# The opening of a decoder step on one core: the third and fourth block of x are read ahead, the first gate weights are cast on VectorE, and two warming products go

## The chip, the cores and the metric

The kernel runs on one NeuronCore of one Trainium2 chip. Time is the device time of one execution in microseconds (us). Three runs of the kernel before gave 2344.27 (the median), 2343.6 and 2344.78 us. One more execution was taken with the hardware profiler; all lines of the profile come from it. Engines are named as the profile names them: PE is TensorE (PEld its weight loads), ACT is ScalarE, DVE is VectorE, POOL is GpSimd, SP is SyncE, which issues most DMAs.

## What is computed

One layer of a hybrid decoder on 304 tokens: 16 meta tokens, 256 of a prompt and 8 x 4 of a sample group. Cut to what matters:

```
def swiglu(x, w_gate, w_up, w_down):
    return (jax.nn.silu(x @ w_gate) * (x @ w_up)) @ w_down

x = x + 0.5 * swiglu(rmsnorm(x, norm_ffn1[l]), ffn1_w_gate[l], ffn1_w_up[l], ffn1_w_down[l])
m, hn, rn, im_ = mixer(rmsnorm(x, norm_mix[l]), l, hists[l], hres[l], hims[l], pos0)
x = x + m
x = x + 0.5 * swiglu(rmsnorm(x, norm_ffn2[l]), ffn2_w_gate[l], ffn2_w_up[l], ffn2_w_down[l])
```

D_MODEL is 2048, the FFN is 5632 wide, all numbers are fp32. The change touches only the start of the first line with `x + 0.5 * swiglu`: the norm of x and the first 256 columns of `x @ w_gate` and `x @ w_up`.

## The kernel before

**Exact products from rounded ones.** Each fp32 operand is split into a high part, rounded to the type fp32r, and a low part, the rest. A product of two such operands is three matmuls on PE: high by high, high by low, low by high (`mm3`, L241 to L243). ACT makes the high parts (for weights `whi`, for x `X` in L302), DVE the low ones (`wlo`, and `X` in L310). Activations lie with features on the 128 partitions and the 304 tokens along the free axis, so x has 16 rows of k ("tiles" of 128 features), four to a block: `pk` holds block 0, `xc1` to `xc3` the others (the profile writes `xc` for all three).

**The stream of weights.** Weights come in pieces of 4 rows of k by 256 columns, 512 KB each, in one fixed order for the whole program. `load` (L130, on SP) reads a piece into a ring of three `raw` slots; `high` (L152, ACT) and `low` (L161, DVE) split it into rings of four buffers; the slot is free when `low` is done, a buffer when PE has used it. `step` does `high`, `low` and `load` for one piece each. Pieces are numbered here in the order in which they are used: in the opening 0, 2, 4, 6 are gate and 1, 3, 5, 7 up; 8 to 11 are the gate weights of the next 256 columns.

**The opening** (`opening`, from L387) begins before anything is on the chip. Its work:

- SP reads `pk` in four transfers, one for each row of k: the norm's gain, the row of x, and pieces 0 and 1 for that row (L394). A part of the first transfer is read by ACT's queue (L396), `vec` too (L398). Then SP reads piece 2, block 1 of x in two halves (L402), pieces 3 and 4, and `hc` (L201).
- `stir` has PE multiply ones by ones STIR times; nothing reads the result. The profile counts two PE instructions for each.
- For each row of `pk`, `norm.add` makes the high and low part of x, and `parted` (L133 to L146) those of the two weight pieces for this row, the high ones with L143 on ACT, the low ones with L144 on DVE. `mms0` (L434) is the first row's 12 matmuls, in the order high by high, high by low, low by high.
- Then come four chunks of 48 matmuls, each a block of x with a gate and an up piece. After each half chunk `norm.add` is called for two rows of the next block, and `step` for the next pieces. Block c + 2 of x is read by SP in chunk c after the gate half (L465), at that place in SP's list.
- `squares` sums the squares of x for the norm: ACT squares a whole block (L418, L421), DVE adds (L422 to L426). PE turns the sums over (`ss`, L340) while the gate weights of the next 256 columns run, after pieces 8 and 9. The result is needed only then, since the norm's factor is multiplied in after the products.

Each engine works through its list in order, so an instruction that waits holds up all behind it. SP's list is such a list too: a read that waits for a `raw` slot holds up every read behind it.

Of the kernel before, what the change touches and what calls it, by code (L numbers as in the profile page):

```python
# [20 lines left out]
KD = D // P  # L21
# [6 lines left out]
NT = NMETA + NPR + NB * NS  # L28
# [4 lines left out]
KC = 4  # L33
# [11 lines left out]
NTV = 16 + NA  # L45
POOLRATE = 3.5
LATE = 8
STIR = 9
LAG = 2
ROWS = 15  # L50
MAGIC = 12582912.0
# [4 lines left out]
GC = 16  # L56
# [19 lines left out]
def nm(g, s):  # L76
    g.uid += 1
    return f"{s}_{g.uid}"
# [35 lines left out]
class Weights:  # L114
# [15 lines left out]
        g.nc.sync.dma_start(self.raw[i], src)  # L130
        self.loaded += 1

    def parted(self, i, k, src=None):  # L133

        nc = self.g.nc
        src = self.raw[i][:, k] if src is None else src
        if k == 0:
            self.parts[i] = tuple(self.pool.tile([P, KC, 256], F32R, tag=x, name=nm(self.g, x), bufs=AHEAD + 2)
                                  for x in ("whi", "wlo"))
            self.nhi += 1  # L140
            self.nlo += 1
        hi, lo = self.parts[i]
        nc.scalar.copy(hi[:, k], src)  # L143
        nc.vector.tensor_tensor(lo[:, k], src, hi[:, k].bitcast(F32), ALU.subtract)  # L144
        if k == KC - 1:
            self.raw.pop(i, None)  # L146
# [47 lines left out]
def tables(g):  # L194
    g.ident = g.const.tile([P, P], F32, name="ident")
    make_identity(g.nc, g.ident)


def masks(g):
    g.hc = g.const.tile([P, NT + NTV], F32, name="hc")  # L200
    g.nc.sync.dma_start(g.hc, g.I["consts"])  # L201
# [7 lines left out]
def step(g):  # L209

    g.w.high()
    flush(g)
    g.w.low()
    g.w.load()
    g.owed += g.rate
    while g.owed >= 1.0:
        g.owed -= 1.0
        got = next(g.side, None) if g.side is not None else None
        if got is None:
            g.side = None  # L220
# [18 lines left out]
def mm3(g, ps, wh, wl, x, start, stop):  # L239
    mm = g.nc.tensor.matmul  # L240
    mm(ps, wh, x[0], start=start, stop=False)  # L241
    mm(ps, wh, x[1], start=False, stop=False)  # L242
    mm(ps, wl, x[0], start=False, stop=stop)  # L243


def warm(g, func, pool=None):

    t = (pool or g.act).tile([P, 16 if pool else 1], F32, tag="warm", name=nm(g, "warm"))
    g.nc.scalar.activation(t[:, :1], g.ones[:, :1], func)


def bank(g, name, aux=False, pool=None):
    return (pool or (g.psaux if aux else g.psum)).tile([P, 512], F32, tag="ps", name=nm(g, name))
# [126 lines left out]
def stir(g):  # L380

    ps = bank(g, "stir", aux=True)
    for _ in range(STIR):
        g.nc.tensor.matmul(ps[:, :P], g.ones, g.ones, start=True, stop=True)


def opening(g, norm, xc, pk, sqp):  # L387

    nc, x, src = g.nc, g.x, g.I["xt"]
    names = ("ffn1_w_gate", "ffn1_w_up")  # L390
    cut = GC + NT + 256
    for k in range(KC):
        c1 = PKW if k else cut
        nc.sync.dma_start(pk[:, k, :c1], g.I["first"][k, :, :c1])  # L394
        if k == 0:
            nc.scalar.dma_start(pk[:, k, cut:], g.I["first"][k, :, cut:])  # L396
    warm(g, AF.Silu, g.const)
    nc.scalar.dma_start(g.vec, g.I["vec"])  # L398
    g.w.loaded = 2
    g.w.load()  # L400
    for h in range(2):
        nc.sync.dma_start(xc[1][:, 2 * h:2 * h + 2], src[1][:, 2 * h:2 * h + 2])  # L402
    g.w.load()
    g.w.load()
    tables(g)
    masks(g)
    stir(g)
    for k in range(KC):
        norm.add(x[k:k + 1], False, gain=pk[:, k, 0:1])
        for i in range(2):  # L410
            g.w.parted(i, k, pk[:, k, GC + NT + 256 * i:GC + NT + 256 * (i + 1)])
    pss = [[bank(g, "pj")[:, :norm.n] for _ in range(2)] for _ in range(2)]
    sums = sqp.tile([P, KC, NT], F32, name="sums")

    def squares(c):

        if c == 0:
            nc.scalar.activation(sums, xc[c], AF.Square)  # L418
            return
        sq = sqp.tile([P, KC, NT], F32, tag="sqs", name=nm(g, "sqs"))  # L420
        nc.scalar.activation(sq, xc[c], AF.Square)  # L421
        nc.vector.tensor_tensor(sums, sums, sq, ALU.add)  # L422
        if c == KD // KC - 1:
            nc.vector.tensor_tensor(sums[:, :2], sums[:, :2], sums[:, 2:], ALU.add)
            norm.acc = sums[:, 0]
            nc.vector.tensor_tensor(norm.acc, sums[:, 0], sums[:, 1], ALU.add)  # L426

    def mms0(ws):

        for w, y in ((0, 0), (0, 1), (1, 0)):  # L430
            for u in range(2):
                for f in range(2):
                    fs = slice(f * P, (f + 1) * P)
                    nc.tensor.matmul(pss[u][f], ws[u][w][:, 0, fs], norm.x[0][y], start=w == y == 0, stop=False)  # L434

    def mms(c, u, ws, kk):
        for f in range(2):
            fs = slice(f * P, (f + 1) * P)
            k = c * KC + kk
            mm3(g, pss[u][f], ws[u][0][:, kk, fs], ws[u][1][:, kk, fs], norm.x[k], k == 0, k == KD - 1)  # L440

    for c in range(KD // KC):
        if c == 0:
            ws = [g.w.take(name, 0, KC, 0) for name in names]
            mms0(ws)
            for kk in range(1, KC):
                for u in range(2):
                    mms(c, u, ws, kk)
        for u in range(2):
            if c:  # L450
                ws = [None, None]
                ws[u] = g.w.take(names[u], c * KC, KC, 0)
                for kk in range(KC):
                    mms(c, u, ws, kk)
            k = (c + 1) * KC + 2 * u
            if k < KD:
                norm.add(x[k:k + 2], False)
            if c == 0 and u == 0:
                for kk in range(KC):
                    g.w.parted(2, kk)  # L460
                g.w.load()
            else:
                step(g)
            if u == 0 and c + 2 < KD // KC:
                nc.sync.dma_start(xc[c + 2], src[c + 2])  # L465
            if c == 3 and u == 0:
                g.w.high()
                g.w.low()
                g.w.load()
            if c and u:  # L470
                squares(c - 1)
    return pss, squares
# [816 lines left out]
def body(ctx, tc, I, O):  # L1289
# [6 lines left out]
    with ExitStack() as c1:  # L1296
        xpool = c1.enter_context(tc.tile_pool(name="xp1", bufs=1))
        fpool = c1.enter_context(tc.tile_pool(name="ffn1", bufs=1))
        g.parts["H"] = (fpool, 4 * FC)
        pk = xpool.tile([P, KC, PKW], F32, name="pk")  # L1300
        xc = [pk[:, :, GC:GC + NT]] + [xpool.tile([P, KC, NT], F32, name=f"xc{c}") for c in range(1, KD // KC)]
        g.x = [xc[m // KC][:, m % KC] for m in range(KD)]
        sqs = ExitStack()
        sqp = sqs.enter_context(tc.tile_pool(name="sqs", bufs=1))
        opened = opening(g, n1, xc, pk, sqp)

        def started():
            sqs.close()
            g.side, g.rate = ssm_setup(g), SETRATE

        late = []

        def done(ms):
            n2.add([g.x[k] for k in ms], late=late if ms[0] >= LATE else None)
            for k in ms:
                nc.gpsimd.dma_start(xsc[k], g.x[k][:, NMETA:])

        g.started = started
        ffn(g, fpool, n1, 1, "H", done, opened)
        flush(g)  # L1320
        drain(g)
        ps0 = proj(g, "w_in", 0, n2.x, NT, KD, lambda c: [late.pop(0)() for _ in range(min(len(late), 2))])
        g.post.append(n2.begin)
# [67 lines left out]
```

## Time and profile before

| | |
|---|---|
| runs, median (lowest, highest) | 2344.27 us (2343.6, 2344.78) |
| profiled execution | 2344.06 us |
| its span, first to last instruction | 2342.3 us |
| PE busy | 2325.2 us, 99% of the span |
| DVE, ACT, POOL busy | 1582.5, 976.8, 87.7 us |
| DMA | 429.98 MB, mean 184 GB/s |

The page gives busy time by engine and groups of instructions by line. The timeline gives, for each row, start and length in us, the engine, line and operation, the tile written and those read, and in brackets how long the engine had been idle and what released it. An "SPq" row is the issue of a DMA, not its transfer. A table by stretch gives for a window the busy time and count of each engine, then PE's clock share, the DMA share and GB/s.

### The profile page before, as it was taken

How to read it: one execution, taken by the hardware profiler on the slowest of the kernel's cores; microseconds unless marked ns; L12 is line 12 of the kernel's file. 1: busy time of each engine (PE TensorE's matmuls, PEld its weight loads, DVE VectorE, ACT ScalarE, POOL GpSimd, SP SyncE). 2: the span in 40 equal slices, each digit the busy share in tenths (PEclk: the TensorE clock that was granted, in tenths of full speed). 3: DMA queues.
4: the chain of work that ended last, by engine and by line, in shares of the span. 5: the costliest groups of instructions: out<-in, count | busy, mean ns of one | idle time of the engine just before them, and what ended most of it. 6: DMA issues, size and time to landing. Idle time of an engine off the chain costs nothing.

```text
span 2342.3 us, 42290 instructions
## 1 busy us (share of the span) xinstructions
PE 2325.2 (99%) x17391; PEld 2306.2 (98%) x17391; DVE 1582.5 (68%) x2415; ACT 976.8 (42%) x1432; POOL 87.7 (4%) x160
## 2 busy tenths in 40 slices
PE   9999999999999999999999999999999999999997
PEld 8999999999999999999999999999999999999997
DVE  6788777877554558699999766555555555555655
ACT  5333433333533335445454544433333333333334
POOL 0000000001000002100000130000000000000000
PEclk9999999999999999999999999999999999999999
DMA  5444555556644445556666674444444444444443
GB/s 210 164 161 172 206 203 206 190 200 200 221 167 161 154 161 206 196 199 224 227 236 212 204 266 162 168 163 170 163 167 167 165 169 164 164 167 167 167 164 111
DMA packets 119361, 429.98 MB, mean 184 GB/s; under 512 B 14532, under 2 KB 19024, under 8 KB 119160
## 3 DMA queue, kind: packets, MB, share of 16 engines
q1 hardware_dynamic: 106800, 375.64, 46.0%
q0 software_dynamic: 12080, 51.45, 6.5%
q8 instruction: 136, 2.23, 0.4%
q14 instruction: 57, 0.47, 0.1%
q10 hardware_dynamic: 288, 0.19, 0.0%
HBM read 397.64 MB, written 29.95 MB: 183 GB/s over the span
## 4 chain that ended last, share of the span: by engine, by line
PE 97%; DMA 1%; DVE 1%; ACT 1%; issue 0%; SPq 0%; ACTq 0%; DVEq 0%
PE pj L241 24%; PE pj L242 24%; PE pj L243 24%; PE dn L243 8%; PE dn L241 8%; PE dn L242 8%; DMA xc<-in_xt 1%; PE bu L896 1%; PE yps L911 1%; DVE wlo L161 0%; DMA raw<-in_ffn_w_gate 0%; ACT whi L152 0%; DVE sums L422 0%; PE ss L340 0%; PE bt L839 0%
## 5 line engine op out<-in xcount | busy, mean ns | idle before, releaser
L161 DVE TENSOR_TENSOR wlo<-raw,whi 128x1024 fp32r<-128x1024 f32 x695 | 848.8, 1222 | 566.6 <-ACT whi L152 564.9
L152 ACT CAST whi<-raw 128x1024 fp32r<-128x1024 f32 x695 | 729.6, 1051 | 1135.5 <-PE pj L242 705.0
L241 PE MATMUL pj<-X,whi 128*128 128x304 f32 (+1 forms) x2428 | 731.3, 301 | 2.1 <-ACT whi L152 1.6
L243 PE MATMUL pj<-X,wlo 128*128 128x304 f32 (+1 forms) x2428 | 727.8, 300 | 1.4 <-DVE wlo L161 1.4
L242 PE MATMUL pj<-X,whi 128*128 128x304 f32 (+1 forms) x2428 | 728.1, 300 | 0.0
L242 PE MATMUL pj<-Y,whi 128*128 128x288 f32 x1728 | 510.2, 295 | 0.0
L241 PE MATMUL pj<-Y,whi 128*128 128x288 f32 x1728 | 510.0, 295 | 0.0
L243 PE MATMUL pj<-Y,wlo 128*128 128x288 f32 x1728 | 509.3, 295 | 0.0
L241 PEld LDWEIGHTS pj<-X,whi 128*128 128x128 f32 x2428 | 457.1, 188 | 8.6 <-issue 5.6
L243 PEld LDWEIGHTS pj<-X,wlo 128*128 128x128 f32 x2428 | 456.4, 188 | 2.2 <-DVE wlo L161 1.9
L242 PEld LDWEIGHTS pj<-X,whi 128*128 128x128 f32 x2428 | 456.6, 188 | 0.0
L241 PEld LDWEIGHTS pj<-Y,whi 128*128 128x128 f32 x1728 | 325.2, 188 | 2.0 <-issue 2.0
L242 PEld LDWEIGHTS pj<-Y,whi 128*128 128x128 f32 x1728 | 325.0, 188 | 0.0
L243 PEld LDWEIGHTS pj<-Y,wlo 128*128 128x128 f32 x1728 | 324.5, 188 | 0.0
L243 PE MATMUL dn<-H,wlo 128*128 128x304 f32 x704 | 213.0, 303 | 0.0
L241 PE MATMUL dn<-H,whi 128*128 128x304 f32 x704 | 213.0, 303 | 0.0
L242 PE MATMUL dn<-H,whi 128*128 128x304 f32 x704 | 212.2, 301 | 0.0
L242 PE MATMUL dn<-X,whi 128*128 128x288 f32 x704 | 207.7, 295 | 0.0
L241 PE MATMUL dn<-X,whi 128*128 128x288 f32 x704 | 207.5, 295 | 0.0
L243 PE MATMUL dn<-X,wlo 128*128 128x288 f32 x704 | 207.4, 295 | 0.0
L242 PEld LDWEIGHTS dn<-H,whi 128*128 128x128 f32 x704 | 132.4, 188 | 0.0
L242 PEld LDWEIGHTS dn<-X,whi 128*128 128x128 f32 x704 | 132.4, 188 | 0.0
(269 smaller groups left out, 1842.0 us busy)
## 6 DMA issues: line engine op xcount, KB each, us to landing
raw<-in_ffn_w_down SPq DMA_DIRECT2D x176, 512.0 KB, 3.5
raw<-in_ffn_w_gate SPq DMA_DIRECT2D x175, 512.0 KB, 3.5
raw<-in_ffn_w_up SPq DMA_DIRECT2D x175, 512.0 KB, 3.5
raw<-in_w_in SPq DMA_DIRECT2D x96, 512.0 KB, 4.0
raw<-in_w_out SPq DMA_DIRECT2D x32, 512.0 KB, 4.0
esc<-ee POOLq DMA_DIRECT2D x16, 912.0 KB, 5.8
ee<-esc POOLq DMA_DIRECT2D x16, 912.0 KB, 6.4
raw<-in_w_branch_a SPq DMA_DIRECT2D x16, 512.0 KB, 3.5
```

The costliest lines, as they stand in the source:

```text
L152: self.g.nc.scalar.copy(hi, self.raw[i])
L161: self.g.nc.vector.tensor_tensor(lo, raw, hi.bitcast(F32), ALU.subtract)
L241: mm(ps, wh, x[0], start=start, stop=False)
L242: mm(ps, wh, x[1], start=False, stop=False)
L243: mm(ps, wl, x[0], start=False, stop=stop)
L896: g.nc.tensor.matmul(ps, self.bs[i][rows, b, ri], self.up[u][rows], start=n == 0, stop=n == 2)
L911: g.nc.tensor.matmul(self.yps[i][q * 32:q * 32 + 32], c[:, h, q], s["k"][h][:, jj, NMETA:], start=k == 0, stop=k == 2)
```

## The change

```
-STIR = 9
+STIR = 7
...
-    def parted(self, i, k, src=None):
+    def parted(self, i, k, src=None, first=False):
...
-        nc.scalar.copy(hi[:, k], src)
+        (nc.vector.tensor_copy if first else nc.scalar.copy)(hi[:, k], src)
...
     g.w.load()
+    nc.sync.dma_start(xc[2], src[2])
     g.w.load()
+    nc.sync.dma_start(xc[3], src[3])
     tables(g)
     masks(g)
     stir(g)
     for k in range(KC):
-        norm.add(x[k:k + 1], False, gain=pk[:, k, 0:1])
+        lows = []
+        norm.add(x[k:k + 1], False, late=lows if k == 0 else None, gain=pk[:, k, 0:1])
         for i in range(2):
-            g.w.parted(i, k, pk[:, k, GC + NT + 256 * i:GC + NT + 256 * (i + 1)])
+            cols = slice(GC + NT + 256 * i, GC + NT + 256 * (i + 1))
+            g.w.parted(i, k, pk[:, k, cols], k == i == 0)
+            for f in lows:
+                f()
+            lows = []
...
-            if u == 0 and c + 2 < KD // KC:
-                nc.sync.dma_start(xc[c + 2], src[c + 2])
```

Three things change. SP reads blocks 2 and 3 of x ahead of pieces 4 and 5. The high part of piece 0's first row is cast by DVE, and its low part is made ahead of that of the first row of x. PE has two warming products fewer, which are four PE instructions in the profile.

SP's list in the opening, before, from piece 3 to piece 8. The names are the kernel's tiles (`raw` a weight piece, 3 to 8 in this order; `xc_104` and `xc_105` blocks 2 and 3 of x), the semaphores DMAHW belong to earlier reads, DVE to the release of a slot:

```order
L130 DMA raw_121<-in_ffn_w_up 128x1024 [waits DMAHW1_49]
L130 DMA raw_123<-in_ffn_w_gate 128x1024 [waits DMAHW2_49]
L201 DMA hc<-in_consts 128x337 [waits DMAHW3_49]
L130 DMA raw_249<-in_ffn_w_up 128x1024 [waits DMAHW6_49,DMAHW4_49,DVE_49]
L465 DMA xc_104<-in_xt 128x1216 [waits DMAHW5_49]
L130 DMA raw_264<-in_ffn_w_gate 128x1024 [waits DMAHW1_49,DVE_49]
L130 DMA raw_302<-in_ffn_w_up 128x1024 [waits DMAHW7_49,DMAHW2_49,DVE_49]
L465 DMA xc_105<-in_xt 128x1216 [waits DMAHW0_49]
L130 DMA raw_341<-in_ffn_w_gate 128x1024 [waits DMAHW4_49,DVE_49]
```

And now:

```order
L130 DMA raw_121<-in_ffn_w_up 128x1024 [waits DMAHW1_49]
L404 DMA xc_104<-in_xt 128x1216 [waits DMAHW2_49]
L130 DMA raw_124<-in_ffn_w_gate 128x1024 [waits DMAHW3_49]
L406 DMA xc_105<-in_xt 128x1216 [waits DMAHW4_49]
L201 DMA hc<-in_consts 128x337 [waits DMAHW5_49]
L130 DMA raw_249<-in_ffn_w_up 128x1024 [waits DMAHW6_49,DVE_49]
L130 DMA raw_263<-in_ffn_w_gate 128x1024 [waits DMAHW7_49,DMAHW1_49,DVE_49]
L130 DMA raw_301<-in_ffn_w_up 128x1024 [waits DMAHW3_49,DMAHW0_49,DVE_49]
L130 DMA raw_339<-in_ffn_w_gate 128x1024 [waits DMAHW6_49,DVE_49]
```

Both blocks of x stand ahead of the first read that waits for DVE. They wait only for a semaphore of an early read: DMAHW2 and DMAHW4 are those on which ACT waits for the second and the third transfer of `pk`. No read of x stands between pieces 5 and 8 any more.

DVE's list at its start, before and now, up to the second row of x (`whi_145` or `whi_146` is piece 0's high part, `whi_150` piece 1's, `X_142` and `X_143` the high and low part of the first row of x):

```order
 L189 MEMSET ones 128x128
+L143 CAST whi_145<-pk 128x256
+L144 TENSOR_TENSOR wlo_146<-pk,whi_145 128x256
 L310 SCALAR_TENSOR_TENSOR X_143<-pk,X_142 128x304
-L144 TENSOR_TENSOR wlo_147<-pk,whi_146 128x256
 L144 TENSOR_TENSOR wlo_151<-pk,whi_150 128x256
 L310 SCALAR_TENSOR_TENSOR X_155<-pk,X_154 128x304
```

The cast is DVE's first work on data, piece 0's low part stands ahead of x's, and ACT, whose list loses the cast, goes from the first row of x straight to piece 1.

## The prediction

> **What bounds the kernel now.** I read the page first, then the busy time by stretch, then what the weight loads of TensorE waited for in the opening, and last the chain of waits behind that.
>
> ```profile
> PE 2325.2 (99%) x17391; PEld 2306.2 (98%) x17391; DVE 1582.5 (68%) x2415; ACT 976.8 (42%) x1432; POOL 87.7 (4%) x160
> ```
>
> TensorE is the bound. The table by stretch (span, then PE, PEld, DVE, ACT, POOL busy) tells where the largest holes lie:
>
> ```profile
> 19.60:23.00 3.40, 1.32 (x7) 0.82 (x7) 2.77 (x5) 3.40 (x7) 0.00 (x0) 1.00 0.07 23
> 29.30:31.00 1.70, 0.92 (x4) 0.67 (x5) 1.65 (x3) 1.70 (x4) 0.00 (x0) 1.00 0.00 0
> 60.00:2343.00 2283.00, 2270.08 (x17025) 2252.58 (x17023) 1541.96 (x2343) 943.06 (x1378) 85.30 (x151) 1.00 0.53 183
> ```
>
> After 60 us there is almost nothing to win; at 19.6 and 29.3 us PE stands still while the DMA engines are nearly idle too (23 and 0 GB/s). So the holes are not a lack of bandwidth: somebody asked late. The timeline of weight loads names the holes (start, length, and in brackets the idle time ahead and its releaser):
>
> ```profile
> 13.12 0.19 PEld L243 LDWEIGHTS pj<-X,wlo 128*128 128x128 f32 x1 [0.22 <-DVE wlo L144]
> 21.23 0.19 PEld L241 LDWEIGHTS pj<-X,whi 128*128 128x128 f32 x1 [1.62 <-ACT whi L152]
> 22.49 0.19 PEld L243 LDWEIGHTS pj<-X,wlo 128*128 128x128 f32 x1 [0.96 <-DVE wlo L161]
> 29.37 0.19 PEld L241 LDWEIGHTS pj<-X,whi 128*128 128x128 f32 x1 [0.44 <-ACT whi L152]
> 30.63 0.19 PEld L243 LDWEIGHTS pj<-X,wlo 128*128 128x128 f32 x1 [0.96 <-DVE wlo L161]
> 44.85 0.74 PEld L340 LDWEIGHTS ss<-ones,sums 128*128 128x128 f32 x6 [1.06 <-PE pj L242]
> ```
>
> ACT and DVE are only the last links. ACT's own timeline shows what they stood behind, and SP's why it came late:
>
> ```profile
> 8.02 0.55 ACT L302 ACTIVATE X<-pk 128x304 fp32r<-128x304 f32 x1 [1.70 <-DMA pk<-in_first]
> 11.17 0.99 ACT L302 ACTIVATE X<-xc,vec 128x304 fp32r<-128x304 f32 x2 [0.93 <-DMA xc<-in_xt]
> 14.17 1.03 ACT L152 CAST whi<-raw 128x1024 fp32r<-128x1024 f32 x1
> 19.26 0.99 ACT L302 ACTIVATE X<-xc,vec 128x304 fp32r<-128x304 f32 x2 [4.05 <-DMA xc<-in_xt]
> 27.38 0.99 ACT L302 ACTIVATE X<-xc,vec 128x304 fp32r<-128x304 f32 x2 [3.25 <-DMA xc<-in_xt]
> ```
>
> ```profile
> 4.44 0.56 SPq L130 DMA_DIRECT2D raw<-in_ffn_w_up  x1
> 5.16 0.55 SPq L130 DMA_DIRECT2D raw<-in_ffn_w_gate  x1
> ...
> 14.10 0.33 SPq L130 DMA_DIRECT2D raw<-in_ffn_w_up  x1
> 14.47 0.43 SPq L465 DMA_DIRECT2D xc<-in_xt  x1
> ...
> 22.84 0.42 SPq L465 DMA_DIRECT2D xc<-in_xt  x1
> ```
>
> In the line left out SP reads the small tile `hc`; then it issues nothing until 14.10 us: weight piece 5 (pieces numbered as loaded; 0 and 1 come inside `pk`) has to wait until DVE has finished with piece 2 and its ring slot is free, and the third block of x, which needs no slot, stands behind it at 14.47. The fourth block stands behind piece 7 until 22.84. ACT has them only at 19.26 and 27.38 (above).
>
> **The change, part by part.**
>
> *The two reads.* They move ahead of weight pieces 4 and 5. Once the third block is there in time, the holes at 21.23 and 22.49 go; with the fourth, those at 29.37 and 30.63; and since ACT and DVE are no longer pushed late, the sums of squares come before PE asks for them, which takes away the hole at 44.85. How much that is, I count twice. First by the idle times: 1.62 + 0.96 + 0.44 + 0.96 + 1.06 = 5.04 us. Then by products:
>
> ```profile
> 13.37 0.30 PE L241 MATMUL pj<-X,whi 128*128 128x304 f32 x1
> 30.87 0.30 PE L241 MATMUL pj<-X,whi 128*128 128x304 f32 x1
> ...
> 43.74 0.30 PE L243 MATMUL pj<-X,wlo 128*128 128x304 f32 x1
> 44.88 0.80 PE L340 MATMUL ss<-ones,sums 128*128 128x2 f32 x6 [0.83 <-DVE sums L426]
> ```
>
> Each chunk (four rows of k, gate and up) is 48 products. From 30.87 (fourth product of the last chunk) to 43.74 (last before `ss`) there are 92 intervals without a wait: 12.87 / 92 = 0.140 us. From 13.37 (fourth product of the second chunk) to `ss` there are 189: 26.4 us, so `ss` would start at 39.8 instead of 44.88, 5.07 us earlier. I take 5.0, for a small part of the 1.06 is the handover itself.
>
> That holds only if nothing else is late, so I follow the supply. Transfers land in the order in which they are issued, at the first row's rate (its last column, GB/s) while the queue is full; the other rows give the time from issue to landing (us, last column) of pieces 3 and 4:
>
> ```profile
> 8.00:12.50 4.50, 4.50 (x34) 4.50 (x33) 3.08 (x8) 3.54 (x10) 0.00 (x0) 1.00 1.02 411
> ```
>
> ```profile
> raw<-in_ffn_w_up SPq DMA_DIRECT2D x1, 512.0 KB, 8.7
> raw<-in_ffn_w_gate SPq DMA_DIRECT2D x1, 512.0 KB, 9.2
> ```
>
> Piece 3 (issued 4.44) lands at 13.1, piece 4 (5.16) at 14.4. At 411 GB/s a piece (512 KB) takes 1.3 us, a block of x (128 x 1216 numbers of 4 bytes) 1.5, `hc` (128 x 337) 0.4. With the change: third block 14.6, piece 4 15.9, fourth block 17.4, `hc` 17.8 (3 us later than now; only the set-up of the scan reads it, which begins after the opening), piece 5 (still issued at 14.10) 19.1. The new reads are not free of waits: in the built program each waits on the semaphore of an early `pk` read; the later of those is the one that ACT received at 8.02, so the fourth block is asked for at some 8.0 us, while the queue is still full until 12.5, and delays nothing but what is named here.
>
> ```profile
> 15.24 1.23 DVE L161 TENSOR_TENSOR wlo<-raw,whi 128x1024 fp32r<-128x1024 f32 x1 [0.28 <-ACT whi L152]
> ```
>
> Third chunk: ACT is done with piece 3 at 15.2, rounds two rows of x by 16.1 and piece 4 by 17.1; DVE ends piece 3 at 16.5 (15.24 + 1.23), the rows at 17.5 (taken as long as ACT's 0.99), piece 4's low part at 18.7. PE asks at 13.37 + 45 x 0.140 = 19.7 for the high and 0.3 later for the low part: 2.6 and 1.3 us to spare. Piece 5: high 19.1 to 20.1, low by 21.3, asked for at 23.0. Fourth chunk: ACT squares block 0 (1.2 us) until 21.3, rounds x until 22.2, then piece 6 (issued once DVE frees piece 3 at 16.5, landed by 20.4) until 23.2, low by 24.4, asked for at 26.4.
>
> ```profile
> 40.72 1.23 ACT sqs L421
> 41.97 1.44 DVE sums L422
> 43.43 0.80 DVE sums L424
> 44.25 0.49 DVE sums L426
> ```
>
> Sums: piece 10's high part needs the buffer that PE frees after the fourth chunk's gate, at 29.7; then 1.0 (its cast), 1.2, a DVE sum of 1.4 behind the low part of that piece (33.4), the last square (34.6), and 1.4 + 0.8 + 0.5: 37.4 us. PE asks at 39.8. So the next late thing is 1.3 us away, and it is piece 4.
>
> *The first cast on DVE, two warming products fewer.* No DVE cast of this shape from SBUF is in the trace. Its nearest row is DVE's subtraction on the same 128x256 tile, 0.42 us, and I take that:
>
> ```profile
> L144 DVE TENSOR_TENSOR wlo<-pk,whi x8: 417/418/420, 4.9 to 10.5; 128x256 fp32r<-128x256 f32 x8
> 3.91 0.55 ACT L302 ACTIVATE X<-pk 128x304 fp32r<-128x304 f32 x1 [1.24 <-DMA pk<-in_first]
> 4.85 2.07 PEld L434 LDWEIGHTS pj<-X,whi 128*128 128x128 f32 x8
> 1.05 4.21 PE L384 MATMUL stir<-ones 128*128 128x128 f32 x18 [1.05 <-DVE ones L189]
> ```
>
> `pk` is there at 3.9, so DVE is done at 4.3 and ACT's row of x at 4.46 (3.91 + 0.55): the first product could start at 4.5 instead of 4.9. Any cast between nothing and 0.55 us ends before ACT's row does; a longer one would delay the first product, up to 0.4 us unfelt. Warming takes (4.85 - 1.05) / 18 = 0.21 us per product of the trace, four go, it ends at 4.0: a gap of 0.4 us opens. The gain of 0.4 us is not kept: rows 2 and 3 of `pk` and the second block still land at 8.0 and 11.1 (both waits of ACT above), and PE meets its low part at 13.12 as before. Taken as 0. Bounds: 0.2 gained if that hole closes as well, and a loss by the clock, below.
>
> *Sum.* Nothing after 45 us is timed by anything but PE's progress. The profiled execution took 2344.06 us: 2344.06 - 5.0 = 2339.06. The median of the runs shown is 0.21 higher: **2339.3 us**. A measurement of this kernel tells 0.2% (4.7 us) from no change, so the forecast lies only just beyond that bound, at 2339.6.
>
> **The rivals.**
>
> *The clock stays low longer.* The weight loads show when it rose:
>
> ```profile
> L434 PEld LDWEIGHTS pj<-X,whi x8: 330/330/333, 4.8 to 6.6; 128*128 128x128 f32 x8
> L434 PEld LDWEIGHTS pj<-X,wlo x4: 187/198/330, 6.8 to 7.4; 128*128 128x128 f32 x4
> ```
>
> 330 ns until 6.9 us, 187 after, after 5.85 us of unbroken work from 1.05. If the gap makes the count begin anew at 4.5, it rises at 10.35. Slow products come every (2.07 - 0.33) / 7 = 0.25 us (the row of eight above). The 12 products of the first row of k then end at some 7.2, of the 36 left in the chunk 12 or 13 are slow (7.2 to 10.35) and 23 or 24 take 0.14: 13.6 us. Now the second chunk's fourth product starts at 13.37, so its first would have at 12.95. That is 0.7 us later; the supply behind it is not, and gives nothing back: 2340.0 us.
>
> Against it: the gap is 0.4 us of 5.8. [...]
>
> *The early reads push the weights late.* If the queue runs slower than I take, a hole at piece 4 or 5 takes the place of the old one. The slow stretch of the trace:
>
> ```profile
> 4.50:6.50 2.00, 2.00 (x10) 2.00 (x10) 1.94 (x5) 1.71 (x5) 0.00 (x0) 1.00 1.02 284
> ```
>
> At 284 GB/s after 13.1 us: third block 15.3, piece 4 17.1, fourth block 19.3, `hc` 19.9, piece 5 21.7; its cast and low part (1.03 + 1.23) end at 24.0, asked for at 23.3: 0.7 us of wait. The squares of block 0 stand behind that cast on ACT and carry the delay into the fourth chunk, so I allow it twice: 1.4. It decides once piece 4 is more than 1.3 us late, and gives 2340.0 to 2340.7; I take 2340.5. Against it: 411 GB/s held for 4.5 us with the same queue.
>
> *Slower than before: instruction delivery.* PE's weight loads also wait without any releaser, all after 60 us:
>
> ```profile
> PEld pj L241 <- issue: 7.6, 30, 0.5
> ```
>
> 7.6 us in 30 places. The change takes instructions out of PE's and ACT's lists and adds one to DVE's, which shifts every later instruction; if those places fall badly and this group doubles, that is 7.6 us against 5.0: 2346.9. It decides from 5.0 us. For it speaks only that the places have no other cause in the trace; against it, that four instructions of 17391 go.
>
> *The change doesn't do what it says:* the reads move, but ACT is not faster, e.g. because a semaphore of theirs is late. Then only part of the holes goes; half is 2341.8.
>
> **How the numbers follow.** All five holes gone 0.70 (by itself 2338.8 to 2339.9, the hole at 13.12 and the spread of the runs); clock 0.10; late weights 0.10; half 0.05; instruction delivery 0.05. The range leaves out the last two and takes in the hole at 13.12 and half of the runs' spread below: 2338.4 to 2341.0. Faster by over 0.2%: three quarters of the first case and a little of the others, 0.57; slower by over 0.2% needs 9.7 us more of instruction waits, 0.02; within 0.2%: 0.41.
>
> **What would show it.** Right: ACT starts on the third block by 16 us and on the fourth by 22 without a DMA wait; no PEld wait over 0.3 us between 13.4 and 40; `ss` at 39.8. The first product at 4.5, and 13.12 unchanged. Wrong: loads of 330 ns after 7 us (clock); a PEld wait on `wlo` at 20 or 23 (weights late); `ss` at 39.8 but a span that is not 5 us shorter (instruction delivery).

## The result, and the profile after

The changed kernel takes 2338.5 us (median of 11 runs, 2338.09 to 2339.84), the kernel before 2343.84 us in the same comparison (11 runs). The ratio is 0.9978 with a 95% interval of 0.9968 to 0.9987: 5.3 us less. The forecast was 2339.3 us, 5.0 less than the median that it started from, with a range of 2338.4 to 2341.0. The result is only 0.1 us above the lower end of that range; the kernel before, too, is 0.43 us below the median that the forecast started from. That the gain is over 0.2% is the likelier side (0.22%), but the interval reaches down to 0.13%.

The page of the profile after, its span and PE:

```profile
span 2337.0 us, 42282 instructions
PE 2323.5 (99%) x17387; PEld 2304.9 (99%) x17387; DVE 1582.9 (68%) x2416; ACT 976.7 (42%) x1431; POOL 87.6 (4%) x160
```

The weight loads of PE that follow idle time, up to the end of the opening, and the first one of `ss`:

```profile
1.05 3.06 PEld L384 LDWEIGHTS stir<-ones 128*128 128x128 f32 x14 [1.05 <-DVE ones L189]
4.43 1.69 PEld L441 LDWEIGHTS pj<-X,whi 128*128 128x128 f32 x8 [0.32 <-ACT X L302]
8.78 0.19 PEld L241 LDWEIGHTS pj<-X,whi 128*128 128x128 f32 x1 [0.42 <-ACT whi L143]
12.95 0.19 PEld L243 LDWEIGHTS pj<-X,wlo 128*128 128x128 f32 x1 [0.20 <-DVE wlo L144]
...
39.46 0.77 PEld L340 LDWEIGHTS ss<-ones,sums 128*128 128x128 f32 x6
```

Between 12.95 and 39.46 there is no row with a wait left: the holes of 1.62, 0.96, 0.44, 0.96 and 1.06 us are gone, all five. SP's list and ACT's starts on the blocks of x show why:

```profile
5.70 0.63 SPq L404 DMA_DIRECT2D xc<-in_xt  x1
6.38 0.56 SPq L130 DMA_DIRECT2D raw<-in_ffn_w_gate  x1
7.88 0.33 SPq L406 DMA_DIRECT2D xc<-in_xt  x1
8.90 0.33 SPq L201 DMA_DIRECT2D hc<-in_consts  x1
13.93 0.33 SPq L130 DMA_DIRECT2D raw<-in_ffn_w_up  x1
```

```profile
11.00 0.99 ACT L302 ACTIVATE X<-xc,vec 128x304 fp32r<-128x304 f32 x2 [0.91 <-DMA xc<-in_xt]
...
14.95 0.98 ACT L302 ACTIVATE X<-xc,vec 128x304 fp32r<-128x304 f32 x2
...
18.95 1.05 ACT L152 CAST whi<-raw 128x1024 fp32r<-128x1024 f32 x1 [1.19 <-DMA raw<-in_ffn_w_up]
...
21.02 0.98 ACT L302 ACTIVATE X<-xc,vec 128x304 fp32r<-128x304 f32 x2
```

The blocks are asked for at 5.70 and 7.88 instead of 14.47 and 22.84. ACT takes them up at 14.95 and 21.02, in its own time and without a wait, where it had waited 4.05 and 3.25 us for the transfers. It now waits for a weight piece instead (18.95, piece 5), but that is early enough for PE.

All of the gain lies in the opening. PE starts on `ss` at 39.59 us instead of 44.88, 5.29 us earlier; from there to the end it is 2297.41 us (2337.0 - 39.59) where it was 2297.42 (2342.3 - 44.88). Within 0.2 us this holds in every trace of this study, so the start of `ss` stands for the whole time below:

| trace | block 1 taken up by ACT at | `ss` starts on PE at | span less that |
|---|---|---|---|
| before | 11.17 | 44.88 | 2297.42 |
| after | 11.00 | 39.59 | 2297.41 |
| only the reads | 10.98 | 39.58 | 2297.42 |
| only cast and warming | 10.46 | 44.64 | 2297.56 |
| only the third block | 10.89; again 10.16 | 40.67; again 40.08 | 2297.53; 2297.42 |
| only the fourth block | 9.97; again 10.66 | 41.32; again 44.86 | 2297.38; 2297.34 |
| one warming product | 10.07 | 40.22 | 2297.38 |
| nine warming products | 10.21 | 39.45 | 2297.35 |
| both blocks ahead of piece 3 | 10.44 | 40.97 | 2297.43 |
| before, again | 9.83 | 43.36 | 2297.44 |
| block 1 ahead of piece 2 | 10.20 | 39.71 | 2297.39 |
| fourth block, PE kept busy | 11.08 | 42.67 | 2297.43 |

The second column is a warning: the same block, asked for at much the same time (only "block 1 ahead of piece 2" asks earlier), is taken up anywhere from 9.83 to 11.17 us, by the same kernel too ("before" twice). A single trace therefore places `ss` only to within about a microsecond where PE waits for data.

### The profile page after: what moved, and what is told of

Same layout as the page of the kernel before. It is cut to its first block, busy times and chain, and to the rows that moved or that the text cites. A ratio compares the mean times of both kernels' runs of the same rounds, so it can differ in the third digit from the quotient of the medians.

```text
span 2337.0 us, 42282 instructions
## 1 busy us (share of the span) xinstructions
PE 2323.5 (99%) x17387; PEld 2304.9 (99%) x17387; DVE 1582.9 (68%) x2416; ACT 976.7 (42%) x1431; POOL 87.6 (4%) x160
## 4 chain that ended last, share of the span: by engine, by line
PE 98%; DVE 0%; ACT 0%; DMA 0%; issue 0%; SPq 0%; ACTq 0%; DVEq 0%
PE pj L241 24%; PE pj L242 24%; PE pj L243 24%; PE dn L243 8%; PE dn L241 8%; PE dn L242 8%; PE bu L901 1%; PE yps L916 1%; DMA pk<-in_first 0%; DVE acc L330 0%; PE bt L844 0%; PE ss L340 0%; ACT y L1277 0%; PE ty L1239 0%; PE rb L356 0%
## 5 line engine op out<-in xcount | busy, mean ns | idle before, releaser
L241 PE MATMUL pj<-X,whi 128*128 128x304 f32 (+1 forms) x2428 | 731.2, 301 | 0.7 <-DVE Y L270 0.5
L241 PE MATMUL pj<-Y,whi 128*128 128x288 f32 x1728 | 510.0, 295 | 0.0
L241 PEld LDWEIGHTS pj<-X,whi 128*128 128x128 f32 x2428 | 457.1, 188 | 6.9 <-issue 5.8
L241 PEld LDWEIGHTS pj<-Y,whi 128*128 128x128 f32 x1728 | 325.2, 188 | 2.1 <-issue 2.0
L241 PE MATMUL dn<-H,whi 128*128 128x304 f32 x704 | 213.0, 303 | 0.0
L241 PE MATMUL dn<-X,whi 128*128 128x288 f32 x704 | 207.5, 295 | 0.0
```

## The experiments

### The two halves of the change

Only the reads, on the kernel before (nine warming products, cast on ACT):

```
     g.w.load()
+    nc.sync.dma_start(xc[2], src[2])
     g.w.load()
+    nc.sync.dma_start(xc[3], src[3])
...
-            if u == 0 and c + 2 < KD // KC:
-                nc.sync.dma_start(xc[c + 2], src[c + 2])
```

> Only the two reads of x move; nine warming products and the cast on ACT stay. My theory: the reads are the whole change, so the first sum of squares on PE (ss) starts at 39.8 us (39.6 to 40.1) as with the full change, the first product at 4.9 instead of 4.4, and the time falls by 4.9 to 5.3 us against the kernel before. Rival, the start counts: the earlier first product (0.5 us) is carried to the end, so this kernel is 0.4 to 0.5 us slower than the full change and ss starts at 40.2 to 40.3.

Measured: 2338.33 us against 2343.32, ratio 0.9978 (0.9969 to 0.9987), the same as the full change; `ss` at 39.58.

The other half, the full change with the reads back at their old place:

```
-    nc.sync.dma_start(xc[2], src[2])
-    nc.sync.dma_start(xc[3], src[3])
...
+            if u == 0 and c + 2 < KD // KC:
+                nc.sync.dma_start(xc[c + 2], src[c + 2])
```

> The other half: seven warming products and the cast on VectorE, the reads of x at their old place. My theory: first product at 4.4, but ss at 44.7 to 44.9 as in the kernel before, time unchanged (within 0.3 us), since the third tile of pk and the second block of x land when they did. Rival, the start counts: ss at 44.4 and 0.4 to 0.5 us faster.

Measured: 2343.92 us against 2343.32, ratio 1.0001 (0.9992 to 1.0010); `ss` at 44.64, a little under the 44.7 expected, in a trace in which block 1 came 0.7 us earlier than in the first one, but PE's granted clock was 0.50 from 22.7 to 26.1 us (more on that with the fourth block below). The reads are the whole gain, and the earlier first product is worth nothing that can be measured: the rival falls on both sides.

### One read at a time

Only the third block is moved:

```
     g.w.load()
+    nc.sync.dma_start(xc[2], src[2])
     g.w.load()
...
-            if u == 0 and c + 2 < KD // KC:
+            if u == 0 and c + 2 == 3:
```

> Only the third block is read ahead; the fourth stays behind piece 7. My theory as the prediction put it (each read owns its holes): the holes at 21.23 and 22.49 go (2.6 us), those before the fourth chunk stay (0.44 and 0.96) and with them some of the 1.06 at ss: ss at 41.2 to 42.3, time 2.6 to 3.6 us below the kernel before. Rival, one chain: with the third block in time DVE frees piece 4 at 18.4 instead of 22.4, so piece 7 and the fourth block are asked for at 18.4 and 18.8, the block lands at 23.3, its piece is cast by 25.2 and low by 26.5, just when PE asks (26.2 and 26.5): no hole over 0.3, ss at 39.8 to 40.1, and the second read brings nothing by itself.

Measured: 2340.72 us (2339.45 to 2342.64) against 2343.32, ratio 0.9989 (0.9980 to 0.9998). So in the median it is 2.6 us faster than before and 2.4 slower than with both reads (2338.33 on the same chip); `ss` at 40.67. SP and PE of that trace:

```profile
18.25 0.33 SPq L130 DMA_DIRECT2D raw<-in_ffn_w_up  x1
18.62 0.42 SPq L466 DMA_DIRECT2D xc<-in_xt  x1
```

```profile
26.77 0.19 PEld L243 LDWEIGHTS pj<-X,wlo 128*128 128x128 f32 x1 [0.46 <-DVE wlo L161]
...
40.64 0.74 PEld L340 LDWEIGHTS ss<-ones,sums 128*128 128x128 f32 x6 [0.75 <-PE pj L242]
```

Neither expectation holds in full. The chain is there: with the third block in time, piece 7 and the fourth block are asked for at 18.25 and 18.62 instead of 22.46 and 22.84, within 0.2 us of what the rival said, and of the fourth block's own holes of 1.4 us some 0.5 are left. But it comes just too late, and `ss` keeps a hole of 0.75. The time lies between the two. I profiled it a second time:

> The kernel with only the third block ahead, profiled a second time: runs from 2339.45 to 2342.64, the profiled one at 2339.93 with holes of 0.46 us at the fourth chunk and 0.75 at ss. Theory, no margin: the fourth block is asked for only when DVE frees piece 4 and lands when its chunk begins, so the holes at the fourth chunk and at ss change with every run, together by the difference in time: 1.2 us of holes at 2339.9, 2 us at 2340.7, 3.5 us at 2342.2. Rival: the spread comes from elsewhere, the holes are 1.2 us again.

Measured: 2339.3 us, holes of 0.65 (at 26.22) and 0.66 us, `ss` at 40.08. The holes are 1.2 to 1.3 us in both traces and the time differs by 0.6: it is block 1, 0.7 us earlier this time, that moved `ss`. Both traces are of executions below the median; what those of 2341 to 2342.6 look like was not seen.

Only the fourth block is moved:

```
     g.w.load()
     g.w.load()
+    nc.sync.dma_start(xc[3], src[3])
...
-            if u == 0 and c + 2 < KD // KC:
+            if u == 0 and c + 2 == 2:
```

> Only the fourth block is read ahead; the third stays behind piece 5. My theory: the holes before the third chunk stay (1.62 and 0.96, perhaps 0.2 longer, since the fourth block now lies on the queue before piece 5), those before the fourth go, and ss is not late: ss at 42.3 to 42.7, time 2.2 to 2.6 us below the kernel before. Rival, one chain: what is late at the third chunk stays late by the same amount to the end, ss at 44.5 or later and under 0.5 us gained.

Measured: 2342.73 us (2340.47 to 2344.05) against 2343.32, ratio 0.9995 (0.9986 to 1.0004): no difference that can be told. The trace, of the fastest of these executions, agrees with my theory (holes of 1.12 and 0.96 us at the third chunk, none later, `ss` at 41.32, early because block 1 was); the median does not. The two holes:

```profile
20.17 0.19 PEld L241 LDWEIGHTS pj<-X,whi 128*128 128x128 f32 x1 [1.12 <-ACT whi L152]
21.43 0.19 PEld L243 LDWEIGHTS pj<-X,wlo 128*128 128x128 f32 x1 [0.96 <-DVE wlo L161]
```

Hence a second trace:

> The kernel with only the fourth block ahead, profiled a second time: its profiled run was its fastest (2340.47 us, median 2342.73), with the second block landing 1.1 us early and ss at 41.2. My theory: with the block at 11.0 or so the holes before the third chunk are 1.6 to 2.0 and 1.0 us, ss at 42.3 to 42.7 and the time at 2341.2 to 2341.8. The runs at 2342.4 to 2344 say that another wait comes in then: one at the fourth chunk or at ss of 1 us or more, from weight pieces 6 to 10, would be the rival (one chain), with ss at 43.2 or later.

Measured: 2343.97 us, `ss` at 44.86. PE's waits after 13 us in this second trace, and then the table by stretch (span, then PE, PEld, DVE, ACT, POOL busy, granted clock, DMA share, GB/s):

```profile
20.93 0.19 PEld L241 LDWEIGHTS pj<-X,whi 128*128 128x128 f32 x1 [1.84 <-ACT whi L152]
22.19 0.29 PEld L243 LDWEIGHTS pj<-X,wlo 128*128 128x128 f32 x1 [0.96 <-DVE wlo L161]
```

```profile
20.00:21.50 1.50, 0.55 (x2) 0.30 (x2) 1.11 (x3) 1.50 (x3) 0.00 (x0) 1.00 0.03 14
22.00:28.00 6.00, 5.80 (x23) 5.81 (x24) 5.47 (x10) 6.00 (x9) 0.00 (x0) 0.50 0.57 181
28.50:36.00 7.50, 7.50 (x56) 7.50 (x55) 4.14 (x5) 3.19 (x5) 0.00 (x0) 1.00 0.73 216
```

No wait comes in after 22.19, and PE is busy all the time, yet from that weight load to `ss` it takes 22.67 us, where the first trace has 19.89 (41.32 - 21.43): 2.8 us more. The granted clock tells: 0.50 from 22 to 28 us, 1.00 around it. In those 6 us PE gets through 23 products, and through 56 in the 7.5 us after. At 0.14 us each, 23 products take 3.2 us; 2.6 of the 5.8 busy us are the clock. By the trace's clock records the clock is at 0.50 from 21.5 to 28.4 us. It falls within the second of two idle stretches of 1.84 and 0.96 us, with two products between them. The rival that I wrote down (a wait from the later pieces) is not what it is.

Two other traces show a fall in the opening, in their tables by stretch. With cast and warming the clock is at 0.50 from 22.7 to 26.1 us, after holes of 1.83 and 0.96 us; in the kernel before a second time from 22.4 to 25.8 us, after 1.47 and 0.96. In the first trace of the kernel before, with holes of 1.62 and 0.96 us, it is at 1.00 in every stretch from 20 to 29 us, and in the first trace of this kernel, with 1.12 and 0.96, too. So the length of the two holes alone doesn't tell whether the clock falls: it stayed up after 1.62 and 0.96 us and fell after 1.47 and 0.96. What else decides was not shown.

If idling is the cause, the same kernel with PE kept at work in that hole must lose its longest times:

```
+                if c == 2 and u == 0:
+                    stir(g, 6)
```

> The kernel with only the fourth block ahead, and six warming products on PE ahead of the third chunk's first product, where PE otherwise stands idle for 1.1 to 1.8 us. They take about 1.3 us at full clock and add no other work. Theory: in the second trace of that kernel PE's clock fell to 0.5 after the two holes (from 21.8 to 28.3 us) and cost 2.7 us, and that is what its runs of 2342 to 2344 us are. With the hole filled the clock stays at 1.00 to the end of the opening, ss starts at 41.2 to 42.7 and the runs lie at 2340.4 to 2341.8, median some 1.3 us below 2342.73. Rival, the clock falls for another reason than the idle time, or the late reads cost the 2 us: the median stays at 2342.4 to 2343.1 and the spread at 3 us or more.

```profile
19.47 1.44 PEld L384 LDWEIGHTS stir<-ones 128*128 128x128 f32 x12
21.45 0.19 PEld L241 LDWEIGHTS pj<-X,whi 128*128 128x128 f32 x1 [0.53 <-ACT whi L152]
22.71 0.19 PEld L243 LDWEIGHTS pj<-X,wlo 128*128 128x128 f32 x1 [0.96 <-DVE wlo L161]
```

Measured: 2341.54 us (2340.7 to 2343.65), median 1.2 us below the same kernel without them. The two were measured on different chips; against the kernel before on the same chip, they gain 2.0 us (2343.58) and 0.6 us (2343.32), and the ratios, 0.9992 (0.9983 to 1.0001) and 0.9995 (0.9986 to 1.0004), overlap widely. In the trace block 1 came late (11.08), `ss` stands at 42.67, and the clock is at 1.00 in every stretch from 20 to 29 us. That is the direction and the size expected, of a kernel that only does more work; but three of the 11 runs are above 2341.8, so the clock is not shown to be the whole of the spread, nor are the runs around the median of the kernel without the six products shown to be those with a fall.

### How many warming products

The full change with one and with nine of them:

```
-STIR = 7
+STIR = 1
```

> The full change, but one warming product instead of seven: PE idles from about 1.5 to 4.4 us. The clock rival of the prediction: the count of work begins anew at 4.4, slow loads (330 ns) until about 10.3, ss 0.7 us later than with the full change (40.4 to 40.6). The opposite: the rise comes at the same place (5.5 to 6.9 us) whatever PE did before, and ss stays at 39.7 to 39.9. If it rises in between (7 to 9 us), the waits for pk at 8.8 and for the second block at 12.9 take up the delay and ss moves by less than 0.3.

```
-STIR = 7
+STIR = 9
```

> The full change with nine warming products: no idle time of PE before the first product, which starts at 4.9 instead of 4.4. My theory: ss at 39.8 as with the full change, time equal within 0.3 us; slow loads until about 6.9 as in the kernel before if the gap or the earlier work with data made the clock rise earlier (5.6 to 5.9 with the full change), anywhere from 5.5 to 6.9 if it differs from run to run.

Measured: with nine 2338.45 us, ratio 0.9978 (0.9969 to 0.9988), the same as with seven. With one 2339.17, ratio 0.9982 (0.9972 to 0.9992): 0.7 us more in the median, with runs and intervals that overlap, so the trace has to tell. PE's weight loads with one warming product:

```profile
4.77 2.02 PEld L441 LDWEIGHTS pj<-X,whi 128*128 128x128 f32 x8 [3.21 <-ACT X L302]
6.71 1.09 PEld L441 LDWEIGHTS pj<-X,wlo 128*128 128x128 f32 x4
...
8.48 0.33 PEld L241 LDWEIGHTS pj<-X,whi 128*128 128x128 f32 x1
8.74 0.23 PEld L242 LDWEIGHTS pj<-X,whi 128*128 128x128 f32 x1
8.92 0.19 PEld L243 LDWEIGHTS pj<-X,wlo 128*128 128x128 f32 x1
```

After 3.2 us of idling the loads stay at 0.33 us until 8.8, and `ss` starts 0.6 us later than with seven although block 1 came 0.9 us earlier. The size is that of the prediction's clock rival (0.7 us); the instant is not, 8.8 instead of 10.3: it rises 4.0 us after work begins, not the 5.85 us that the rival took.

### One place earlier, and block 1 first

Both reads ahead of piece 3:

```
-    g.w.load()
     nc.sync.dma_start(xc[2], src[2])
-    g.w.load()
     nc.sync.dma_start(xc[3], src[3])
+    g.w.load()
+    g.w.load()
```

> The full change with both reads one place earlier still, ahead of weight piece 3. Theory, the queue is served in order: the second block still lands at 11.0, the two blocks at 13.3 and 14.9, piece 3 at 16.2 instead of 13.1; PE asks for it at 16.1, its cast is done at 17.2 and its low part at 18.5: two new holes of 1.1 and 1.0 us between 16 and 19, ss at 41.6 to 42.1, 1.9 to 2.3 us slower than the full change. Rival, transfers share the engines: the second block lands late (12.5 or more), the hole at 12.95 grows to 1.5 or more and piece 3 is less late.

```profile
16.42 0.19 PEld L241 LDWEIGHTS pj<-X,whi 128*128 128x128 f32 x1 [0.93 <-ACT whi L152]
17.68 0.19 PEld L243 LDWEIGHTS pj<-X,wlo 128*128 128x128 f32 x1 [0.96 <-DVE wlo L161]
```

ACT waits for piece 3:

```profile
15.32 1.04 ACT L152 CAST whi<-raw 128x1024 fp32r<-128x1024 f32 x1 [1.79 <-DMA raw<-in_ffn_w_up]
```

Measured: 2340.4 us, ratio 0.9986 (0.9977 to 0.9996), 1.9 us above the full change. Two new holes of 0.93 and 0.96 us, near what was priced (1.1 and 1.0); block 1 is not late (10.44), only piece 3 is (its cast starts at 15.32, after the full change at 14.01). That is what a queue served in order gives and not what the rival said, so here the place of each read decides which wait it makes: at the old place the reads are late, one place earlier than now the weights.

Block 1 of x ahead of piece 2, in the full change:

```
     g.w.loaded = 2
-    g.w.load()
     for h in range(2):
         nc.sync.dma_start(xc[1][:, 2 * h:2 * h + 2], src[1][:, 2 * h:2 * h + 2])
+    g.w.load()
```

> The full change, and block 1 of x read ahead of weight piece 2. Theory: block 1 lands about 1.3 us earlier (9.7 instead of 11.0 us, less in a run with a faster start), piece 2 lands at 11.0 and is cast then, the hole at 12.95 (0.2 us) goes, PE runs without a wait from the third row of pk on, ss at 39.3 to 39.6, 0.1 to 0.3 us faster than the full change, which a measurement cannot tell. Rival: piece 2 is now late by more than the block is early, the hole grows (PE waits for the high part at 12.5 or later), ss at 40 or later.

Measured: 2338.2 us (2337.78 to 2339.5), ratio 0.9978 (0.9969 to 0.9987): not to be told from the full change. ACT takes block 1 up at 10.20 without a wait and the hole at 12.95 is gone, but one of 0.19 us stands at 16.42 and the one at 8.8 stays (0.44); `ss` at 39.71, a little later than the 39.3 to 39.6 expected.

### The kernel before, a second time

> The kernel before, profiled a second time, since the time at which the second block of x lands went from 9.9 to 11.1 us among the traces. If that is a matter of the run (the DMA rate between 4 and 6.5 us went from 285 to 362 GB/s), this trace shows another landing than 11.1 us for the same kernel, and ss moves with it: 44.88 minus the time that the block is earlier. If it belongs to the kernel, the block lands within 0.2 us of 11.1 and ss starts at 44.7 to 45.0.

Measured: 2342.61 us, with block 1 at 9.83 (the transfers between 4.5 and 6.5 us ran at 357 GB/s; 284 in the first trace) and `ss` at 43.36: a matter of the run. There is more in it:

```profile
20.00:22.00 2.00, 1.27 (x7) 1.02 (x8) 2.00 (x3) 2.00 (x4) 0.00 (x0) 1.00 0.00 0
22.50:25.50 3.00, 3.00 (x14) 3.00 (x13) 0.75 (x1) 0.42 (x1) 0.00 (x0) 0.50 0.99 347
```

Here too the clock falls to 0.50 after the holes at the third chunk (1.47 and 0.96 us), and the holes at the fourth, 0.44 and 0.96 us in the first trace, are not there. Slow products fill the time in which PE would have waited for the fourth block anyhow. `ss` moves by 1.52 us, block 1 by 1.34. So a fall of the clock cost this execution of the kernel before next to nothing; with only the fourth block moved, there is no such wait left to hide it.

## Why the prediction was right, and where it was not

- **Holes and their sum (5.0 us): right.** From 13.20 (the fourth product of the second chunk after the change) to `ss` at 39.59 are 26.39 us; 26.4 was forecast. The gain of 5.29 us is 5.12 of that and 0.17 because block 1 came 0.17 us earlier in this trace, which has nothing to do with the change.
- **Which read takes away which hole: only partly right.** The prediction gave the holes at the third chunk to the third block and those at the fourth to the fourth. Together they are right. But the third read alone already has the fourth block asked for 4.2 us earlier, and the fourth alone gains only 0.6 us in the median, which can't be told from nothing. In one of its two traces PE's clock fell at the hole that is left and cost 2.8 us; that this is what holds its median up is likely and not shown. The sum of the two parts (2.6 and 0.6 us) is not the 5.0 of both.
- **Supply: right.** Third block expected to land at 14.6, piece 4 at 15.9, the fourth block at 17.4. From issue to landing the trace has 8.7, 9.3 and 9.3 us: 14.4, 15.7 and 17.2.
- **Sums of squares: mis-sized, without effect.** They were to be ready at 37.4 us. DVE ends them at 38.3:

```profile
30.61 1.05 ACT L152 CAST whi<-raw 128x1024 fp32r<-128x1024 f32 x1 [1.80 <-DMA raw<-in_ffn_w_gate]
```

```profile
37.83 0.48 DVE L433 TENSOR_TENSOR sums<-sums 128x304 f32<-128x304 f32 x1
```

  Piece 10 was taken to wait for its buffer, until 29.7; it waits for its own transfer, until 30.6. PE asks at 39.5, so 1.2 us remain, not 2.4. Piece 4's low part is done at 18.3 and asked for at 19.8 (13.20 + 45 x 0.140, and 0.3), 1.5 us later, so the sums and not piece 4 would be late next:

```profile
17.11 1.22 DVE L161 TENSOR_TENSOR wlo<-raw,whi 128x1024 fp32r<-128x1024 f32 x1
```

- **Cast and warming: right that they are worth nothing.** The cast takes 0.29 us instead of the 0.42 assumed; the gap ahead of the first product is 0.32, not 0.4; the first product starts at 4.43 as forecast (4.5). The lead is given back at 8.78, in a wait of 0.42 us for the third row of `pk`.

```profile
3.83 0.29 DVE L143 CAST whi<-pk 128x256 fp32r<-128x256 f32 x1 [2.83 <-DMA pk<-in_first]
```

- **The clock rival did not come.** With the gap of 0.32 us the loads of the first eight products are at 0.188 us before the eighth is done, and the clock records put the rise at 5.7 us, earlier than in the kernel before (7.1; the prediction read 6.9 from the loads). The instant is not the change's doing: without any gap it lay at 6.9 with nine products and the cast on DVE, and at 5.3 in the second trace of the kernel before, so for one kernel it was 7.1 in one trace and 5.3 in another. The rival's price was a little too low, too: 12 products 0.25 us apart from 4.5 on end at 7.5 and not at 7.2, which makes the loss 0.8 us and not 0.7.
- **The queue rival did not come** at this place, but one place earlier it did (0.93 and 0.96 us). The margin at piece 4 was 1.5 us in the trace where 1.3 was named; at piece 3, with 3 us of transfers put in front of it, it was used up.
- **Instruction delivery:** PE's waits without releaser at L241 are 7.8 us in 31 places after the change, 7.6 in 30 before. It did not move.

Open: why the DMA rate between 4.5 and 6.5 us is 284 GB/s in one execution of the kernel before and 357 in another, with the DMA engines busy throughout in both (shares of 1.02 and 0.99). Block 1 came 1.3 us earlier in the faster one; the cause was not tried.

## What to carry to other kernels

When PE waits while the DMA engines idle, look in the issuing queue for a transfer that needs nothing but stands behind one that waits for a buffer, and move it ahead; then work out what it delays on the queue, for one place too early cost 1.9 of the 5 us here. Price a set of reads together: the gains of each alone do not add up to that of both. Short holes in PE's work can cost more than their length: in three traces the clock was at 0.50 at or after two of them, for 3.4 to 6.8 us in which PE's row looks busy, and in one of these that took some 2.6 us more.

## What the runs showed of the hardware

- The clock of PE fell to 0.50 at, or within 1.2 us after, two idle stretches close together: of 1.84 and 0.96 us for 6.8 us, of 1.83 and 0.96 and of 1.47 and 0.96 for 3.4 us. After 1.62 and 0.96 us, in the first trace of the kernel before, it did not fall. What decides was not shown.
- The rise at the start came between 4.0 and 7.1 us in the 13 traces with seven or nine warming products, and at 8.8 after 3.2 us of idling. The column of the granted clock shows 1.00 before the rise all the same (4.5 to 6.5 us in the kernel before, with loads of 0.33 us): the weight loads, 0.33 or 0.188 us, are what to read.
- Transfers into SBUF ran at 402 to 415 GB/s from 8 to 10.5 or 12.5 us, with the DMA engines busy throughout (shares of 1.02 to 1.05, 12 traces).
- A cast from fp32 to fp32r of 128x256 took DVE 0.29 us, ACT 0.39.
